# Retention's projections paced over the steps of the RWKV recurrence, and its states passed through DRAM

## The chip, the cores and the metric

One core of a Trainium2 chip runs one program. The metric is its device time in microseconds (us). PE, DVE, ACT, POOL and SP are the core's five instruction queues: TensorE (matmuls), VectorE, ScalarE, GpSimd and SyncE (which here only issues DMAs). Each queue runs its instructions in the order in which the program holds them, and an instruction that waits holds up everything behind it on its queue.

## The reference, cut to what matters

The whole computation is two transformer blocks. The change touches one layer of the second block, for 1024 latent rows and 256 context rows with 8 heads of 64. Two mixers start from the same normalised input `h`:

```python
u = h @ w_in                      # projections of every mixer, 1024 columns in
# retention, both directions: chunks of 128 rows, decay g per head
kv = einsum('bhnsd,bhnse->nbhde', kc * k_decay, vc)
s_next = g_chunk * s + kv_n       # state before each chunk: 64 x 64 per head
y = (q k^T * dmat) v + (q * q_decay) s_prev
# RWKV-7, both directions, row after row
s = s * w_t + (s @ -kk_t) (kk_t * a_t)^T + v_t k_t^T ;  y_t = s r_t
# combine: norm of each, times silu(u[gate columns]), then @ w_out
```

## The kernel before

All matrix products with weights are float32 work done as three matmuls on split operands (`mm3`, lines 217 to 219): `hi` and `lo` parts of the input, `hhi`/`hlo`, against those of the weights, `whi`/`wlo`. The input has three blocks of rows: blocks 0 and 1 hold 512 latent rows each, block 2 the 256 context rows. One projection of 8 depth slices is 24 matmuls: 256 columns wide in `proj_tm` (128 rows of input against 256 weight columns), 512 wide in `proj_fm` for blocks 0 and 1, 256 wide for block 2. Their PSUM tiles are called `pf` in this stage.

`mixers` runs the stage. `rwkv` is written first: the recurrence as 10 batches, each of two directions with two chunks of 64 rows, so 40 steps in all. For a batch `prep2` builds the operands (`wkr`, `wbk`, `wam`), `invert` inverts unit triangular matrices on DVE in 31 pairs of operations (`wtm`, lines 1670 and 1671) between two trips through DRAM (`wlt`, `wrd`), `merge` joins the halves (matmuls at lines 1694 and 1701), and `chain` makes the four steps. A step is five groups of 8 small matmuls (lines 1746, 1753, 1767, 1779, 1784), with ACT, DVE and POOL between them; its first is at line 1746, and its result leaves by `wyt` (line 1787). The operands of batch b+2 use the buffers of batch b, so the last part of `prep2` of b+2 waits for the end of the chain of b, and so in turn `invert`, `merge` and the chain of b+2.

Written behind it, and so of lower priority, is retention: `ret_proj` for block 0, 1 and 2 (60 projections for k, v and q, 24 for the gates `zt`), then `ret_state`: a table of decays (`rdm`), and for ten chunks the products k v for 8 heads (line 1370) and the two state recurrences on POOL (lines 1382, 1383), all kept in SBUF in one tile `rS`. A scheduler places the instructions of each queue by its own estimate of times and by priority, so the projections land between the steps of the recurrence wherever it believes PE to be free. Only one block of the input fits in SBUF here; the tiles of a new block are loaded from DRAM (line 1508) when the old one is done. After the recurrence `mix_tile` runs for ten tiles of 128 rows (loads of q, k, v at lines 1394 to 1398, transposes at line 1409).

Of the kernel before, what the change touches and what calls it, by code (L numbers as in the profile page):

```python
# [21 lines left out]
P = 128  # L22
# [17 lines left out]
class Ker:  # L40
# [1222 lines left out]

    def ret_proj(self, p, blocks):
# [55 lines left out]
    def ret_state(self, p, pl):  # L1320
# [3 lines left out]
        lg = p.tile([P, 16], F32, name="rlg")  # L1324
# [3 lines left out]
        tc_ = p.tile([P, 8], F32, name="rtc")  # L1328
        nc.sync.dma_start(tc_, a["c_rtc"])
        qdec = p.tile([P, 8, 2], F32, name="rqdec")  # L1330
        kdec = p.tile([P, 8, 2], F32, name="rkdec")
        gch = p.tile([P, 8], F32, name="rgch")
        for dd in range(2):
            l8 = lg[:, 8 * dd:8 * dd + 8]
            nc.vector.tensor_scalar(qdec[:, :, dd], l8, tc_[:, dd:dd + 1], None, op0=OP.mult)
            nc.vector.tensor_scalar(kdec[:, :, dd], l8, tc_[:, 2 + dd:3 + dd], None, op0=OP.mult)
            rows = slice(64 * dd, 64 * dd + 64)
            nc.scalar.activation(gch[rows], lg[rows, 8 * dd:8 * dd + 8], AF.Exp, scale=128.0)
# [3 lines left out]
        dm = p.tile([P, 8, P], F32, name="rdm")  # L1342
        rel = pl.tile([P, 4, P], F32, name="rrel", tag="rrel", bufs=1)
        nc.sync.dma_start(rel, a["c_rrel"])
        for h in range(8):
            e2 = pl.tile([P, 2, P], F32, name="re2", tag="re2", bufs=2)
# [3 lines left out]
            nc.gpsimd.tensor_add(dm[:, h], e2[:, 0], e2[:, 1])  # L1350

        S_ = p.tile([P, 10, 8, 64], F32, name="rS")
        nc.gpsimd.memset(S_[0:64, 8], 0.0)
        nc.gpsimd.memset(S_[64:128, 9], 0.0)

        nxt = [{8: 9, 9: 0}, {9: 8, 8: 7}]
        for t in range(7):
            nxt[0][t] = t + 1
            nxt[1][t + 1] = t
        for t in [8, 9] + list(range(8)):  # L1360
            k = pl.tile([P, 8, 64], F32, name="rkl", tag="rkl", bufs=2)
            nc.sync.dma_start(k, k_d[t].rearrange("p (h d) -> p h d", d=64))
            v = pl.tile([P, 512], F32, name="rvl", tag="rvl", bufs=2)
            nc.sync.dma_start(v, v_d[t])
            kd = pl.tile([P, 8, 2, 64], F32, name="rkd", tag="rkd", bufs=2)
            for dd in range(2):
                nc.gpsimd.tensor_mul(kd[:, :, dd], k, kdec[:, :, dd:dd + 1].to_broadcast([P, 8, 64]))
            ps = self.pf()
            for h in range(8):
                nc.tensor.matmul(ps[:, 64 * h:64 * h + 64], kd[:, h].rearrange("p a d -> p (a d)"),  # L1370
                                 v[:, 64 * h:64 * h + 64], start=True, stop=True)
            for dd in range(2):
                rows = slice(64 * dd, 64 * dd + 64)
                if t in nxt[dd]:
                    nc.scalar.copy(S_[rows, nxt[dd][t]].rearrange("p h d -> p (h d)"), ps[rows])
        for dd, t0 in ((0, 8), (1, 9)):
            rows = slice(64 * dd, 64 * dd + 64)
            t = t0
            while t in nxt[dd]:
                n = nxt[dd][t]  # L1380
                tm = pl.tile([P, 8, 64], F32, name="rtm", tag="rtm", bufs=2)
                nc.gpsimd.tensor_mul(tm[rows], S_[rows, t], gch[rows, :, None].to_broadcast([64, 8, 64]))
                nc.gpsimd.tensor_add(S_[rows, n], S_[rows, n], tm[rows])
                t = n
        self.rt = qdec, dm, S_

    def mix_tile(self, p, pe, t, cat, cv):
# [3 lines left out]
        qdec, dm, S_ = self.rt  # L1391
# [6 lines left out]
        nc.sync.dma_start(v, self.rv_d[t])  # L1398
        yield
# [28 lines left out]
        for h in range(8):  # L1428
            o = y[:, 64 * h:64 * h + 64]
            nc.tensor.matmul(o, sD[:, h % 2, h // 2], v[:, 64 * h:64 * h + 64], start=True, stop=False)  # L1430
            nc.tensor.matmul(o, qdT[:, h], S_[:, t, h], start=False, stop=True)
# [56 lines left out]
    def mixers(self):  # L1488
# [6 lines left out]
        with self.pool("rwm") as p, self.pool("rpb") as pb:  # L1495
# [4 lines left out]
            self.ret_tables(pb)  # L1500
            self.kept = {}
            for b in range(3):
                if b:
                    n = 512 if b < 2 else 256
                    hT = tuple(self.hA.tile([P, KD, 512], F32R, name="h" + x, tag=f"h{x}", bufs=1)[:, :, :n]
                               for x in ("hi", "lo"))
                    for t, src in zip(hT, self.nT_d[b]):
                        self.nc.sync.dma_start(t.bitcast(F32), src)
                    self.nT[b] = hT
                self.ret_proj(pb, [b])  # L1510

            self.close_all("wp", "hA")
            ers = ExitStack()
            rst = ers.enter_context(self.pool("rst", side=self.ms))
            with self.pool("rsl", side=self.ms) as pl:
                self.ret_state(rst, pl)
# [4 lines left out]
        with ers, self.pool("ret") as pr:  # L1521
# [3 lines left out]
            cat = [self.alloc_hT(b) for b in range(3)]  # L1525
            with self.pool("eop") as pe:
# [21 lines left out]
    def rwkv(self, p):  # L1548
        nc, a, dr = self.nc, self.a, self.dr
        d_ = self.rwd  # L1550
        ordt = [[8, 9] + list(range(8)), [9, 8] + list(range(7, -1, -1))]
# [166 lines left out]
        def chain(d, m, end):  # L1718
# [4 lines left out]
            for n, c in enumerate(cs):  # L1723
# [19 lines left out]
                for i in range(4):  # L1743
                    for e in range(2):
                        o = 512 * (1 - e) + 64 * i
                        nc.tensor.matmul(u[RW[e], o:o + 64], am[c][:, e, i, 0:64], xv[:, i, e],
                                         start=True, stop=True, tile_position=(0, 64 * e))
# [890 lines left out]
```

## Time and profile before

| | us |
|---|---|
| three timed runs | 4215.55, 4213.84, 4200.82 |
| their median | 4213.84 |
| the profiled execution | 4202.26 |
| its span | 4199.8 |

The profile is of one further execution. The span runs from its first to its last instruction, and the 2.5 us around it are start and end. The stage of the change lies from about 2099 us to 2934 us of the span: the recurrence's first step begins at 2248.4 us, its last result is stored at about 2928 us, and `mix_tile` follows. A time such as 2248.4 is always counted from the start of the span.

### The profile page before, as it was taken

The numbers are of one execution on the slowest core, as the hardware profiler recorded it, in microseconds if no ns is written. First come the engines' busy times: TensorE is split into PE (matmuls) and PEld (weight loads), VectorE is DVE, ScalarE is ACT, GpSimd is POOL, SyncE is SP. The second block draws the span as 40 slices with busy tenths as digits, with TensorE's granted clock in tenths as the row PEclk, the third lists the DMA queues.
The fourth block names the chain that finished last, engine by engine and source line by source line (L and its number), as shares of the span: only waits on it lengthen the run. The fifth ranks groups of instructions, "written<-read, shape, count | busy, mean of one in ns | idle before, by whom it ended". The sixth has DMA issues, their size and how long they took to land. (4 is left out here: it accounts for less than half of the span.)

```text
span 4199.8 us, 59342 instructions
## 1 busy us (share of the span) xinstructions
PE 3812.9 (91%) x23289; PEld 3077.8 (73%) x23289; DVE 2130.2 (51%) x3284; ACT 1320.4 (31%) x2641; POOL 1129.9 (27%) x1153
## 2 busy tenths in 40 slices
PE   7999989988999999789879899887889999998997
PEld 4788877776878788667767687776567877776775
DVE  4232434447343434644337686665556427653576
ACT  4333332215312121442233333332224224332211
POOL 1110202123101011202256343236431200003674
PEclk8999979998999999988989999876899999998998
DMA  5321227573141413333477655653754644324465
GB/s 201 123 100 67 98 84 264 189 263 118 50 148 63 147 50 129 126 125 122 138 229 221 187 161 173 206 157 99 234 188 142 225 134 125 102 70 152 165 203 193
DMA packets 453574, 627.03 MB, mean 149 GB/s; under 512 B 142577, under 2 KB 302499, under 8 KB 447152
## 3 DMA queue, kind: packets, MB, share of 16 engines
q1 hardware_dynamic: 402816, 421.50, 31.1%
q0 software_dynamic: 50480, 201.75, 14.5%
q8 instruction: 184, 3.01, 0.3%
q14 instruction: 94, 0.77, 0.1%
HBM read 427.27 MB, written 195.19 MB: 148 GB/s over the span
## 5 line engine op out<-in xcount | busy, mean ns | idle before, releaser
L217 PE MATMUL p<-hhi,whi 128*128 128x512 f32 x1056 | 415.8, 394 | 5.9 <-DVE hf L389 5.8
L218 PE MATMUL p<-hlo,whi 128*128 128x512 f32 x1056 | 414.3, 392 | 4.3 <-DVE hlo L391 4.3
L219 PE MATMUL p<-hhi,wlo 128*128 128x512 f32 x1056 | 413.8, 392 | 0.0
L217 PE MATMUL pf<-whi,hhi 128*128 128x512 f32 (+1 forms) x992 | 359.0, 362 | 29.4 <-ACT rqr L1279 9.4
L218 PE MATMUL pf<-wlo,hhi 128*128 128x512 f32 (+1 forms) x992 | 352.4, 356 | 3.7 <-DVE wlo L177 3.4
L177 DVE TENSOR_TENSOR wlo<-wraw,whi 128x2048 fp32r<-128x2048 f32 (+1 forms) x103 | 212.3, 2062 | 273.8 <-ACT whi L176 267.8
L219 PE MATMUL pf<-whi,hlo 128*128 128x512 f32 (+1 forms) x992 | 349.3, 353 | 0.0
L176 ACT CAST whi<-wraw 128x2048 fp32r<-128x2048 f32 (+1 forms) x123 | 193.2, 1575 | 459.6 <-PE pt L219 174.7
L217 PE MATMUL pf<-hhi,whi 128*128 128x512 f32 (+1 forms) x640 | 252.4, 394 | 6.0 <-DVE zt L1311 2.1
L218 PE MATMUL pf<-hlo,whi 128*128 128x512 f32 (+1 forms) x640 | 252.0, 394 | 0.0
L219 PE MATMUL pf<-hhi,wlo 128*128 128x512 f32 (+1 forms) x640 | 249.4, 390 | 0.0
L217 PEld LDWEIGHTS pf<-whi,hhi 128*128 128x128 f32 x992 | 198.7, 200 | 68.2 <-issue 14.1
L217 PE MATMUL pj<-whi,hhi 128*128 128x512 f32 (+1 forms) x560 | 216.5, 389 | 26.5 <-ACT whi L176 12.1
L217 PEld LDWEIGHTS p<-hhi,whi 128*128 128x128 f32 x1056 | 200.4, 190 | 54.1 <-DVE hf L389 6.2
L218 PEld LDWEIGHTS p<-hlo,whi 128*128 128x128 f32 x1056 | 200.2, 190 | 46.3 <-DVE hlo L391 5.3
L219 PEld LDWEIGHTS p<-hhi,wlo 128*128 128x128 f32 x1056 | 200.0, 189 | 42.6 <-issue 0.8
L218 PEld LDWEIGHTS pf<-wlo,hhi 128*128 128x128 f32 x992 | 198.9, 200 | 28.9 <-issue 4.1
L219 PE MATMUL pj<-whi,hlo 128*128 128x512 f32 (+1 forms) x560 | 214.1, 383 | 3.0 <-DVE hlo L381 3.0
L218 PE MATMUL pj<-wlo,hhi 128*128 128x512 f32 (+1 forms) x560 | 215.1, 384 | 0.2 <-DVE wlo L177 0.2
L219 PEld LDWEIGHTS pf<-whi,hlo 128*128 128x128 f32 x992 | 198.5, 200 | 22.1 <-issue 1.3
L1670 DVE TENSOR_TENSOR wtm<-wT,wL 128x2 f32<-128x2 f32 (+30 forms) x310 | 145.7, 470 | 37.5 <-POOL wL L1661 28.0
L217 PEld LDWEIGHTS pf<-hhi,whi 128*128 128x128 f32 x640 | 122.9, 192 | 37.9 <-issue 6.7
(750 smaller groups left out, 8544.6 us busy)
## 6 DMA issues: line engine op xcount, KB each, us to landing
wraw<-w_in POOLq DMA_DIRECT2D x25, 1024.0 KB, 6.0
wraw<-w_ada POOLq DMA_DIRECT2D x24, 1024.0 KB, 8.5
wraw<-w_up POOLq DMA_DIRECT2D x22, 1024.0 KB, 6.0
whi<-wkh POOLq DMA_DIRECT2D x40, 512.0 KB, 5.6
wlo<-wkl POOLq DMA_DIRECT2D x40, 512.0 KB, 5.2
wraw<-ada_w POOLq DMA_DIRECT2D x32, 512.0 KB, 4.5
ox<-x SPq DMA_DIRECT2D x48, 256.0 KB
xp<-xl SPq DMA_DIRECT2D x48, 256.0 KB
```

Of the source, the lines that this page charges most:

```text
L176: nc.scalar.copy(hi[:, :n], raw[:, :n])
L177: self.we.tensor_sub(lo[:, :n], raw[:, :n], hi[:, :n].bitcast(F32))
L217: mm(out, L[0], R[0], start=first, stop=False)
L218: mm(out, L[0], R[1], start=False, stop=False)
L219: mm(out, L[1], R[0], start=False, stop=last)
L1670: nc.vector.tensor_mul(tv, T[:, r0:, i:], L[:, i:i + 1, i:].to_broadcast([P, 16 - r0, n]))
```

## The change

- In `rwkv` the first matmul of each step is remembered in `self.marks` (40 of them).
- `paced` gives each projection of retention an edge on PE's queue: it may not stand before a given step's first matmul. The steps are dealt out by the sum of assumed durations (2.9 for a projection that is 256 wide, 5.45 for 512): the first 70 us of them are free, the rest is spread evenly over the 40 steps.
- The gates leave `ret_proj` and become `ret_gates`, which runs after k, v and q of all blocks, over blocks 2, 1, 0. Between gate projections `ret_state` advances by one round.
- `ret_state` handles four heads at a time: two passes of nine rounds. A round loads k and v of two chunks from DRAM (four DMAs), scales k on POOL, makes 8 pairs of head and direction as 64 x 64 matmuls, multiplies the state on POOL and adds on DVE; each state goes to DRAM by two DMAs. The table `rdm` goes through DRAM as well.
- `mix_tile` loads its chunk's state (256 KB), and the table once.
- `ctx_norm` stores block 0 of the input to DRAM too, since the gates need it again at the end: two more reloads.

```diff
@@ ctx_norm
-        for b in (1, 2):
+        for b in range(3):
@@ ret_proj and what was its end
+    def paced(self, us):
+        n = int((self.filled - self.lead) / self.pace)
+        self.filled += us
+        return self.tc.issue_after(self.marks[min(n, len(self.marks) - 1)]) if n >= 0 else nullcontext()
...
-                self.proj_tm(self.nT, W, 256, mk(dst, c0), tiles)
+                for t in tiles:
+                    with self.paced(2.9):
+                        self.proj_tm(self.nT, W, 256, mk(dst, c0), [t])
+
+    def ret_gates(self, p, blocks):
...
-                self.proj_fm(self.nT, W, c, ev_z((c0 + c) // P), blocks)
+                for b in blocks:
+                    with self.paced(5.45 if b < 2 else 2.9):
+                        self.proj_fm(self.nT, W, c, ev_z((c0 + c) // P), [b])
+                    yield
@@ ret_state
+        self.st_d = [self.dr.tile([P, 2, 256], F32, name=f"rst{t}") for t in range(10)]
+        for g in range(2):
+            S_ = pl.tile([P, 4, 64], F32, name="rS", tag="rS", bufs=2)
+            for n in range(10):
+                for dd in range(2):
+                    rows = slice(64 * dd, 64 * dd + 64)
+                    nc.sync.dma_start(self.st_d[order[dd][n]][rows, g], S_[rows].rearrange("p h d -> p (h d)"))
+                k = pl.tile([P, 2, 4, 64], F32, name="rkl", tag="rkl", bufs=1)
+                v = pl.tile([P, 2, 256], F32, name="rvl", tag="rvl", bufs=1)
+                for x, x_d in ((k.rearrange("p a h d -> p a (h d)"), k_d), (v, v_d)):
+                    for dd in range(2):
+                        nc.sync.dma_start(x[:, dd], x_d[order[dd][n]][:, 256 * g:256 * g + 256])
+                nc.gpsimd.tensor_mul(k, k, kdec[:, :, 4 * g:4 * g + 4, None].to_broadcast([P, 2, 4, 64]))
+                for h in range(4):
+                    for dd in range(2):
+                        nc.tensor.matmul(ps[64 * dd:64 * dd + 64, 64 * h:64 * h + 64], k[:, dd, h],
+                                         v[:, dd, 64 * h:64 * h + 64], start=True, stop=True, tile_position=(0, 64 * dd))
+                nc.gpsimd.tensor_mul(tm, S_, gch[:, 4 * g:4 * g + 4, None].to_broadcast([P, 4, 64]))
+                nc.vector.tensor_add(S_, tm, ps[:, :256].rearrange("p (h d) -> p h d", d=64))
+                yield
@@ mix_tile
+        S_ = p.tile([P, 8, 64], F32, name="rSl", tag="rSl", bufs=3)
+        nc.sync.dma_start(S_, self.st_d[t].rearrange("p g (h d) -> p (g h) d", d=64))
@@ mixers
+            self.filled, self.lead, self.pace = 0.0, 70.0, 215.0 / len(self.marks)
...
+            with self.pool("rzb") as pb, self.pool("rsl") as pl:
+                steps = self.ret_state(pl)
+                for b in (2, 1, 0):
+                    if b < 2:
+                        block(b)
+                    for _ in self.ret_gates(pb, [b]):
+                        next(steps, None)
+                self.run(steps)
@@ rwkv, chain
+                        if not i and not e:
+                            self.marks.append(mm.ins)
```

What this does to the order of instructions is shown at three places. The first is PE's queue in batch 0, from the first matmuls of its second step on (line 1746 before, 1774 in the changed kernel). Names without a number are tiles of the recurrence; `pf` are retention's projections. Before:

```order
L1746 MATMUL p_14598<-wxv,wam 64x64 x8
L217 MATMUL pf<-hhi,whi 128x512
L218 MATMUL pf<-hlo,whi 128x512
L217 MATMUL pf<-hhi,whi 128x512
L218 MATMUL pf<-hlo,whi 128x512
L219 MATMUL pf<-hhi,wlo 128x512
L217 MATMUL pf<-hhi,whi 128x512
```

and now:

```order
L1774 MATMUL p_14599<-wxv,wam 64x64 x8
L1774 MATMUL p_14659<-wxv,wam 64x64 x8
L1664 MATMUL pj<-ident,wbk 128x128 x4
L1670 MATMUL pj<-wkr,wbk 128x128 x4
L1783 MATMUL p_14599<-wrs,wX_0_13939 64x64 x8
L1783 MATMUL p_14659<-wrs,wX_0_13941 64x64 x8
L1797 MATMUL p_14599<-wxv,wbt 64x64 x8
L1797 MATMUL p_14659<-wxv,wbt 64x64 x8
```

Before, 19 projection matmuls stood between the first matmuls of two neighbouring steps; now the two steps stand next to each other and no projection is between them.

The second place is PE's queue at the end of the recurrence: its last two groups (lines 1779 and 1784 before, 1809 and 1814 now) and what follows. Before:

```order
L1753 MATMUL p_20019<-wrs,wX_1_13941 64x64 x8
L1779 MATMUL p_20019<-wS,wrr 64x64 x8
L1784 MATMUL p_20019<-wxv,wam 64x64 x8
L405 MATMUL pf<-ident,colr 128x8
L282 MATMUL pa<-wraw,cT_7260 32x512 x2
L1409 MATMUL pf<-ident,rql 128x128 x4
```

and now:

```order
L219 MATMUL pf<-hhi,wlo 128x512
L217 MATMUL pf<-hhi,whi 128x512
L1809 MATMUL p_20020<-wS,wrr 64x64 x8
L1814 MATMUL p_20020<-wxv,wam 64x64 x8
L218 MATMUL pf<-hlo,whi 128x512
L219 MATMUL pf<-hhi,wlo 128x512
L217 MATMUL pf<-hhi,whi 128x512
```

Before, the transposes of `mix_tile` (line 1409) followed the last step; now 98 projection matmuls, all 512 wide, stand between the last step and them.

The third place is POOL's queue where the rounds of `ret_state` begin (`rkl` and `rtm` are the round's, `wfc` and `wS` are what a step of the recurrence needs from POOL). Before, the rounds stood behind one another near the end:

```order
L1367 TENSOR_TENSOR rkd<-rkl,rkdec 128x8x64 x2
L1383 TENSOR_TENSOR rS<-rS,rtm 64x512
L1661 MEMSET wL 128x32
L1382 TENSOR_TENSOR rtm<-rS,rgch 64x512
L1367 TENSOR_TENSOR rkd<-rkl,rkdec 128x8x64 x2
L1383 TENSOR_TENSOR rS<-rS,rtm 64x512
```

and now:

```order
L1762 TENSOR_TENSOR wfc<-wfi 128x4
L1383 TENSOR_TENSOR rtm<-rS,rgch 128x256
L177 TENSOR_TENSOR wlo<-wraw,whi 128x1024
L1376 TENSOR_TENSOR rkl<-rkl,rkdec 128x512
L165 DMA wraw<-even_w_in 128x8x128
L1767 TENSOR_TENSOR wS<-wt_17687,wfc 128x256
L1767 TENSOR_TENSOR wS<-wt_17749,wfc 128x256
L1762 TENSOR_TENSOR wfc<-wfi 128x4 x2
```

The scaling of the loaded k (line 1376, which waits for its DMA) now stands ahead of operations that steps of the recurrence wait for (lines 1762 and 1767).

## Rows read from the trace of the kernel before

**Rows 1.** Busy time by stretch: batches 0 to 7, batch 8, batch 9, mix_tile.

```profile
core 0: us, PE busy (x) PEld busy (x) DVE busy (x) ACT busy (x) POOL busy (x), PEclk, DMA share, GB/s
2248.40:2842.90 594.50, 524.17 (x5929) 450.17 (x5928) 419.06 (x892) 221.63 (x571) 238.25 (x380) 0.90 0.61 182
2842.90:2907.00 64.10, 49.48 (x593) 45.70 (x592) 45.86 (x88) 16.95 (x38) 49.92 (x46) 0.54 0.26 67
2907.00:2928.00 21.00, 13.54 (x288) 11.76 (x288) 8.74 (x17) 6.63 (x18) 8.09 (x10) 0.86 0.22 61
2934.00:3100.00 166.00, 144.59 (x1111) 100.52 (x1111) 101.34 (x174) 47.97 (x90) 84.87 (x88) 0.86 0.72 226
```

**Rows 2.** The same, instructions that touch pf tiles alone: batches 0 to 7, batch 8.

```profile
2248.40:2842.90 594.50, 286.50 (x1567) 237.99 (x1566) 14.37 (x24) 29.68 (x68) 0.90 0.61 182
2842.90:2907.00 64.10, 25.54 (x113) 24.34 (x112) 0.00 (x0) 8.11 (x14) 0.54 0.26 67
```

**Rows 3.** Lines 1787, 1670, 1686, 1746, 1787: ns (min/median/max), first and last start.

```profile
L1787 ACT COPY wyt<-p x2: 360/364/367, 2450.9 to 2451.3; 64x256 f32<-64x256 f32 x2
...
L1670 DVE TENSOR_TENSOR wtm<-wT,wL x31: 160/292/730, 2471.6 to 2511.4; 128x2 f32<-128x2 f32 x1, 128x3 f32<-128x3 f32 x1, 128x8 f32<-128x8 f32 x1, 128x10 f32<-128x10 f32 x1
...
L1686 SPq DMA_DIRECT2D wV<-wrd x8: 303/448/1837, 2522.0 to 2529.4; - x8
...
L1746 PE MATMUL p<-wxv,wam x64: 222/222/347, 2536.6 to 2577.1; 128*64 128x64 f32 x64
...
L1787 ACT COPY wyt<-p x8: 348/366/367, 2549.3 to 2593.5; 64x256 f32<-64x256 f32 x8
```

**Rows 4.** Line 1746 in batches 0, 8 and 9, and line 1787 in batch 9.

```profile
L1746 PE MATMUL p<-wxv,wam x64: 222/222/369, 2248.4 to 2295.5; 128*64 128x64 f32 x64
...
L1746 PE MATMUL p<-wxv,wam x64: 314/314/369, 2842.9 to 2899.9; 128*64 128x64 f32 x64
...
L1746 PE MATMUL p<-wxv,wam x64: 222/222/369, 2907.0 to 2922.3; 128*64 128x64 f32 x64
...
L1787 ACT COPY wyt<-p x8: 365/366/367, 2914.2 to 2927.7; 64x256 f32<-64x256 f32 x8
```

**Rows 5.** Chain of waits by line, as a share of 2250:2770 and of 2840:2928.

```profile
by line: DVE wtm L1670 9.0%; DVE wT L1671 6.4%; DMA wV<-wrd 6.1%; DMA wlt<-wam 5.8%; PE pf L217 5.8%; PE pf L218 5.2%; PE pf L219 5.1%; issue 4.4%; PE pj L1642 3.7%; DMA wrd<-wT 3.5%; DVE wam L1644 3.3%; DVE wxv L1738 2.6%; DMA hhi<-nTd2h 2
...
by line: DVE wtm L1670 26.1%; DVE wT L1671 12.4%; PE p L1779 7.0%; PE p L1784 7.0%; DMA wrd<-wT 4.9%; DVE wt L1772 4.9%; issue 4.2%; PE pf L1370 4.1%; SPq L1686 4.0%; PE p L1753 3.4%; PE p L1767 3.2%; DMA rvl<-rv 3.0%; ACT wyt L1787 2.5%; D
```

**Rows 6.** Timeline of PE: neighbouring projection matmuls, 512 and 256 wide (start, us).

```profile
2629.10 0.40 PE L218 MATMUL pf<-hlo,whi 128*128 128x512 f32 x1
2629.34 0.39 PE L219 MATMUL pf<-hhi,wlo 128*128 128x512 f32 x1
...
2362.68 0.28 PE L218 MATMUL pf<-wlo,hhi 128*128 128x256 f32 x1
2362.79 0.28 PE L217 MATMUL pf<-whi,hhi 128*128 128x256 f32 x1
```

**Rows 7.** Operations of ret_state by line; then one step group on the timeline.

```profile
L1370 PE MATMUL pf<-rvl,rkd x160: 421/421/476, 2824.6 to 2892.9; 128*128 128x64 f32 x160
...
L1367 POOL TENSOR_TENSOR rkd<-rkl,rkdec x20: 1040/1048/1375, 2818.4 to 2881.8; 128x512 f32<-128x512 f32 x20
...
L1383 POOL TENSOR_TENSOR rS<-rS,rtm x18: 1254/1262/1521, 2837.9 to 2911.6; 64x512 f32<-64x512 f32 x18
...
2633.26 0.64 PE L1746 MATMUL p<-wxv,wam 128*64 128x64 f32 x16
```

**Rows 8.** PE waiting for a reloaded block (timeline); a load in the chain of waits.

```profile
2644.91 0.55 PE L217 MATMUL pf<-whi,hhi 128*128 128x256 f32 x1 [5.80 <-DMA hhi<-nTd2h]
...
2886.86 2.64 DMA rvl<-rv
```

**Rows 9.** The loads and first transposes of mix_tile.

```profile
L1394 SPq DMA_DIRECT2D rql<-rq x10: 320/354/613, 2929.3 to 3042.2; - x10
...
L1409 PE MATMUL pf<-ident,rql x40: 272/273/476, 2933.1 to 3061.5; 128*128 128x128 f32 x40
```

More of the change, by code (lines that the diff above doesn't have):

```diff
@@ L1 @@
 import math
-from contextlib import ExitStack
+from contextlib import ExitStack, nullcontext
 import numpy as np
@@ L1349, in ret_state @@
             nc.gpsimd.tensor_mul(e2, e2, rel[:, 2:4])
[L1350 to L1385, printed above, removed]
+            dm = pl.tile([P, P], F32, name="rdm", tag="rtm", bufs=1)
+            nc.gpsimd.tensor_add(dm, e2[:, 0], e2[:, 1])
+            nc.sync.dma_start(self.dm_d[:, h], dm)
+        self.qdec = qdec
     def mix_tile(self, p, pe, t, cat, cv):
         nc = self.nc
-        qdec, dm, S_ = self.rt
+        qdec, dm = self.qdec, self.dm
         py = lambda: self.ps.tile([P, 512], F32, name="py", tag="py", bufs=2)
@@ L1430, in mix_tile @@
             nc.tensor.matmul(o, sD[:, h % 2, h // 2], v[:, 64 * h:64 * h + 64], start=True, stop=False)
-            nc.tensor.matmul(o, qdT[:, h], S_[:, t, h], start=False, stop=True)
+            nc.tensor.matmul(o, qdT[:, h], S_[:, h], start=False, stop=True)
         cols = slice(t * P, t * P + P)
@@ L1494, in mixers @@
         self.open_ps(2)
-        with self.pool("rwm") as p, self.pool("rpb") as pb:
+        with self.pool("rwm") as p:
             self.rwkv(p)
@@ L1499, in mixers, with block @@
             self.we = self.nc.gpsimd
-            self.ret_tables(pb)
             self.kept = {}
[L1502 to L1510, printed above, removed]
+            self.filled, self.lead, self.pace = 0.0, 70.0, 215.0 / len(self.marks)
+            def block(b):
+                n = 512 if b < 2 else 256
+                hT = tuple(self.hA.tile([P, KD, 512], F32R, name="h" + x, tag=f"h{x}", bufs=1)[:, :, :n]
+                           for x in ("hi", "lo"))
+                for t, src in zip(hT, self.nT_d[b]):
+                    self.nc.sync.dma_start(t.bitcast(F32), src)
+                self.nT[b] = hT
+            with self.pool("rpb") as pb:
+                self.ret_tables(pb)
+                for b in range(3):
+                    if b:
+                        block(b)
+                    self.ret_proj(pb, [b])
+            with self.pool("rzb") as pb, self.pool("rsl") as pl:
+                steps = self.ret_state(pl)
+                for b in (2, 1, 0):
+                    if b < 2:
+                        block(b)
+                    for _ in self.ret_gates(pb, [b]):
+                        next(steps, None)
+                self.run(steps)
             self.close_all("wp", "hA")
[L1513 to L1516, printed above, removed]
         self.ms, self.ss = "left", "right"
@@ L1520, in mixers @@
         self.open_ps(2, 1)
-        with ers, self.pool("ret") as pr:
+        with self.pool("ret") as pr:
             self.open_hA()
@@ L1525, in mixers @@
             cat = [self.alloc_hT(b) for b in range(3)]
+            self.dm = pr.tile([P, 8, P], F32, name="rdml")
+            self.nc.sync.dma_start(self.dm, self.dm_d)
             with self.pool("eop") as pe:
@@ L1550, in rwkv @@
         d_ = self.rwd
+        self.marks = []
         ordt = [[8, 9] + list(range(8)), [9, 8] + list(range(7, -1, -1))]
@@ L1745, in chain @@
                         o = 512 * (1 - e) + 64 * i
-                        nc.tensor.matmul(u[RW[e], o:o + 64], am[c][:, e, i, 0:64], xv[:, i, e],
-                                         start=True, stop=True, tile_position=(0, 64 * e))
+                        mm = nc.tensor.matmul(u[RW[e], o:o + 64], am[c][:, e, i, 0:64], xv[:, i, e],
+                                              start=True, stop=True, tile_position=(0, 64 * e))
+                        if not i and not e:
+                            self.marks.append(mm.ins)
                 rs = p.tile([P, 256], F32, name="wrs", tag=f"wrs{d}", bufs=1)
```

28 lines of the change are left out of this document (18 added, 10 removed).

## The prediction

> **What bounds the kernel now.** I read the busy time by stretch first, then the order of instructions, then single lines of the recurrence. In batches 0 to 7 PE is busy for 524 of 594.5 us at a granted clock of 0.90, so nearly always; tiles `pf`, retention's, take 286 us of it [rows 1, 2]. DVE is busy for 419. In batch 8 the projections are over: the clock is 0.54 (PE runs mostly at 1.2 GHz), and the state work of retention takes 25.5 of PE's 49.5 us, while POOL is busy for 50 of 64 [rows 1, 2]. Batch 9 takes 21 us with nothing beside it.
>
> The recurrence itself is a loop over two batches, since the operands of batch b+2 wait for the end of the chain of b. One pass of it: the chain of batch 2 ends at 2451.3 + 0.4 = 2451.7; the inversion for batch 4 starts at 2471.6 and its last product at 2511.4; its result is back in SBUF after loads issued until 2529.4; the first step begins at 2536.6 and the last result leaves at 2593.5 + 0.4 = 2593.9 [rows 3]. That is 142 us for two batches: 20 for the rest of the preparation and its trip through DRAM, 40 of inversion, 25 of trips and joining, 57 for the chain. The chain alone needs no more than 2928 - 2907 = 21 us, as batch 9 shows [rows 4]; in batch 4 it takes 57, because projections and other batches' work stand between its instructions. The chain of waits agrees: in 2250:2770 the three lines of projections have 5.8 + 5.2 + 5.1 = 16% of 520 us, 84 us or some 12 us of each of the 7.2 batches, and the inversion's two lines another 15% [rows 5]. So fill on PE costs the recurrence time, but not as much as it lasts (286 / 8 = 36 us a batch).
>
> **Part by part.** All sums start from the profiled execution, 4202.3 us.
>
> Prices first. At the full clock a 512-wide projection matmul follows the last after 0.23 us, a 256-wide one after 0.11 [rows 6]; with 24 of them a projection takes 5.5 or 2.75 us. A state matmul of the new form (64 x 64) has the shape of a step's: 8 in 0.64 us, so 0.08 each, where the old form with 128 weight columns costs 2 x 0.23 at the low clock (16 profiled rows or 8 matmuls in 3.7 us) [rows 7].
>
> *Batches 0 to 7.* I counted in the listings what stands on PE between the first matmul of a batch's chain and its last. Before: 342 matmuls 512 wide and 859 256 wide, 342 x 0.23 + 859 x 0.115 = 177 us. Now: 59 and 855, and 71 state matmuls, 13.6 + 98.3 + 5.7 = 118 us. The difference is 60 us. What stands between two chains hardly changes (42 and 275 before, 37 and 279 now). Each chain lies in one of two interleaved loops, the even batches' and the odd ones', so a microsecond taken out of a chain moves the end by about half a microsecond. I take **-30**. If the fill is not on the path at all it is 0; if PE's time alone counted it would be -60.
>
> *Batch 8.* The old state work goes: 25.5 us of PE at the low clock, and on POOL most of 20 x 1.05 + 18 x 1.26 = 44 us for `rkd` and `rS` alone, spread from 2818 to 2912 [rows 7]. In comes fill: 96 x 0.23 + 40 x 0.08 = 25 us. The rest of PE's work, 24 us at 0.54, shrinks to some 13 with the clock held up. PE then has 38 instead of 49.5 us of work: **-10**, bounds -20 (POOL was the brake) and +15 (fill goes on top as it does on an idle path).
>
> *Batch 9.* It had no fill; now 94 projection matmuls (94 x 0.23 = 21.6 us) and 16 state matmuls (1.3 us) stand among its steps. PE was idle for 21 - 13.5 = 7.5 us [rows 1], which hides some: **+17**, bounds +14 and +24.
>
> *After the last step.* 98 matmuls follow, 98 x 0.23 = **+22**. Nothing covers them: the loads and transposes of `mix_tile` stand behind them (before, the first load was issued at 2929.3, the first transpose ran at 2933.1 [rows 9]), and its tiles lie where weights and input of the projections lay. Their evacuation and store add the same few microseconds that the recurrence's last store had, so I count no more.
>
> *Reloads.* Four blocks are loaded instead of two. One reload before held PE for 5.80 us [rows 8], and PE's order puts the recurrence behind it. Two more: **+6**, bounds 0 and 12. The extra store of block 0 falls in a stretch where nothing is bound by DMA; I count 0, and at most 4 MB at the 226 GB/s of [rows 1], 18 us, if the next weights queue behind it.
>
> *State rounds.* 18 rounds, each 6 DMAs on SP, 1.05 us on POOL for k [rows 7] and about half that for the state, one addition on DVE. POOL's scaling waits for a load and stands ahead of `wfc` and `wS`, for which the next step's DVE and PE work waits. A load of this kind that was waited for took 2.64 us [rows 8]. If all 18 waits fell on the path: 18 x 2.64 = 48; if all rounds lie in gaps: 0. Loads are issued well ahead in most rounds, so I stay near the low end: **+5**.
>
> *mix_tile.* Ten more loads of 256 KB and a table of 512 KB: 3.1 MB, at 226 GB/s 14 us of DMA. DMA is at 0.72 there and PE busy for 145 of 166 us [rows 1], so most is covered, except at the start, when everything is loaded at once: **+4**, bounds 0 and 14.
>
> Sum: -30 - 10 + 17 + 22 + 6 + 5 + 4 = **+14 us**. The profiled execution, 4202.3, lies near the low end of what was timed; the mean of it and the three runs is 4208.1. With +14 that is **4222 us**, 0.2% above the median of 4213.8. A difference of 0.5% (21 us) is about what a measurement of this kernel can tell from no change, so I forecast none that is clear.
>
> **The rivals.**
>
> *A, faster: PE's own time is the bound.* PE busy for 88% of batches 0 to 7 [rows 1] speaks for it: then each microsecond of fill that leaves a batch shortens the batch by as much, the total of fill is unchanged, and the stage gains the idle and half-clock time of its tail. Batches 0 to 7 give -60 instead of -30 and batch 8 -15: 4222 - 35 = 4187 us. Against it: batch 8, with less PE work than any before it, still took 64 us. Chance 0.22. [...]
>
> *B, slower: latency is the bound, not fill.* If the loop of inversion, trips and DVE queue sets the pace (the inversion alone is 40 of the 71 us that a batch has in the pass of [rows 3], and batch 8, free of projections, still took 64), then the first term is 0 and the fill at the end is paid in full: 4222 + 30 = 4252 us. It decides, with a clear loss, once the first term is smaller than 17 of its 30 us. Against it: 16% of the chain of waits is fill [rows 5]. Chance 0.23.
>
> *C, slower: the rounds of retention hold POOL and SP.* Every round's wait on the path, +48 instead of +5: 4265 us. For it: in-order queues, and one buffer each for k and v. Against it: they are loaded while PE works on other things. Chance 0.10.
>
> That the change does nothing is excluded: the listings show the projections moved.
>
> **How the numbers follow.** My forecast has 0.40, A 0.22, B 0.23, C 0.10, and 0.05 is for what I have not seen. Around the forecast the terms' bounds leave about 4200 to 4244. The range that leaves out 2 in 10 goes from a little below A to B and most of C: 4182 to 4262. Faster by over 0.5% (below 4193) are most of A and little else: 0.22. Slower by over 0.5% (above 4235) are most of B, nearly all of C and an eighth or more of the forecast's own: 0.37. Between them 0.41.
>
> **What the changed kernel's profile would show.** Batches 0 to 7 tell most: 594.5 / 8 = 74.3 us each before; right at about 70.5, A at 67 or less, B at 74. Batch 8 at a clock above 0.85 and below 64 us; batch 9 at some 38 us; then 22 us of projections with PE busy throughout, and the first transpose some 5 us behind. Waits of POOL's line 1376 for `rkl` that add up to over 20 us would speak for C. I am wrong if a batch stays at 74 us, or falls below 66.

## The result and the profile after

The changed kernel takes **4266.69 us** (median of 4 runs, 4263.14 to 4267.92) beside 4210.68 for the kernel before: ratio **1.0137, 95% interval 1.0121 to 1.0153**, slower by 1.4%. The forecast was 4222, its range 4182 to 4262.

Busy time by stretch in the changed kernel, as in [rows 1]: batches 0 to 7, batch 8, batch 9, from the last result to `mix_tile`'s first load, and 166 us of `mix_tile`.

```profile
core 0: us, PE busy (x) PEld busy (x) DVE busy (x) ACT busy (x) POOL busy (x), PEclk, DMA share, GB/s
2255.10:2852.40 597.30, 500.48 (x5771) 434.32 (x5770) 418.55 (x886) 206.47 (x538) 223.07 (x355) 0.81 0.59 173
2852.40:2907.40 55.00, 47.91 (x622) 38.71 (x624) 40.64 (x101) 11.95 (x30) 15.14 (x23) 0.84 0.66 205
2907.40:2957.50 50.10, 43.76 (x465) 34.71 (x462) 10.54 (x22) 12.16 (x33) 14.16 (x22) 0.87 0.57 194
2957.50:2985.80 28.30, 22.26 (x89) 16.73 (x88) 3.51 (x6) 4.37 (x9) 7.93 (x15) 0.96 0.63 209
2985.80:3151.80 166.00, 145.69 (x1014) 102.77 (x1015) 90.85 (x150) 44.09 (x83) 77.17 (x84) 0.81 0.76 238
```

The same for tiles `pf` alone in batches 0 to 7 and in batch 9, as in [rows 2].

```profile
2255.10:2852.40 597.30, 226.46 (x1407) 195.48 (x1406) 10.56 (x23) 20.33 (x52) 0.81 0.59 173
2907.40:2957.50 50.10, 29.81 (x145) 21.69 (x142) 3.15 (x6) 1.77 (x3) 0.87 0.57 194
```

Batches 0 to 7 hold 60 us less of `pf` work (226 against 286) and last as long as before. The clock fell with that work, from 0.90 to 0.81, and PE's other work there grew from 524 - 286 = 238 to 500 - 226 = 274 us: 36 of the 60 us came back at once.

Batch 8 came out as forecast (55 us against 64 before). In batch 9 whole projections stand between the groups of a step. PE's timeline there:

```profile
2937.02 0.64 PE L1774 MATMUL p<-wxv,wam 128*64 128x64 f32 x16
2937.59 0.50 PE L217 MATMUL pf<-hhi,whi 128*128 128x512 f32 x1
...
2942.71 0.39 PE L218 MATMUL pf<-hlo,whi 128*128 128x512 f32 x1
2943.03 0.68 PE L1783 MATMUL p<-wrs,wX 64*64 64x64 f32 x16
```

Behind the last projection PE waits for `mix_tile`'s first load (timeline of PE; line 1423 is the transpose of [rows 9]):

```profile
2981.63 0.39 PE L219 MATMUL pf<-hhi,wlo 128*128 128x512 f32 x1
2981.95 0.22 PE L405 MATMUL pf<-ident,colr 8*128 8x8 f32 x1
2989.68 1.12 PE L1423 MATMUL pf<-ident,rql 128*128 128x128 f32 x4 [7.52 <-DMA rql<-rq]
```

POOL's scaling of k (line 1376) in 2607:2960, first its duration, then its waits:

```profile
L1376 POOL TENSOR_TENSOR rkl<-rkl,rkdec x18: 1036/1045/1583, 2644.4 to 2932.3; 128x512 f32<-128x512 f32 x18
its engine sat idle before it (us, times) until:
  DMA rkl<-rk: 32.4, 8
```

The spans differ by 4265.0 - 4199.8 = 65.2 us: first step later by 6.7, batches 0 to 7 +2.8, batch 8 -9.1, batch 9 +29.1, from the last result to `mix_tile`'s first load +27.0, from there to the end +8.7.

### The profile page after: what moved, and what is told of

Its sections match the earlier page's. It is cut to its first block, busy times and chain, and to the rows that moved or that the text cites. A ratio compares the mean times of both kernels' runs of the same rounds, so it can differ in the third digit from the quotient of the medians.

```text
span 4265.0 us, 59783 instructions
## 1 busy us (share of the span) xinstructions
PE 3857.0 (90%) x23417; PEld 3111.9 (73%) x23417; DVE 2134.2 (50%) x3302; ACT 1309.8 (31%) x2623; POOL 1090.5 (26%) x1133
## 3 DMA queue, kind: packets, MB, share of 16 engines
q1 hardware_dynamic: 417104, 444.58, 32.1%
## 5 line engine op out<-in xcount | busy, mean ns | idle before, releaser
L217 PEld LDWEIGHTS p<-hhi,whi 128*128 128x128 f32 x1056 | 200.5, 190 | 54.6 <-DVE hf L389 6.8
L218 PEld LDWEIGHTS p<-hlo,whi 128*128 128x128 f32 x1056 | 200.2, 190 | 46.2 <-DVE hlo L391 5.3
L218 PEld LDWEIGHTS pf<-wlo,hhi 128*128 128x128 f32 x992 | 202.4, 204 | 32.1 <-issue 4.8
```

Of the source, the lines that this page charges most:

```text
L217: mm(out, L[0], R[0], start=first, stop=False)
L218: mm(out, L[0], R[1], start=False, stop=False)
```

## The experiments

The label of a run stands for the edit that is shown with its expectation below. The stretches are read from the first starts of the chain's and `rql`'s lines and the end of the last `wyt` in each run's trace. "to mix" is from the last result to `mix_tile`'s first load (negative: the load came first), "rest" from there to the end. Stretches are of one execution each; where the code is the same, batches 0 to 7 still vary by some 10 us (two executions of the changed program: 597 and 592), and "rest" by 16 (e14 and e16 are one program: 1276 and 1292), so a difference of a few us there means nothing. The traces of e15 and e16 are of their shortest and longest execution (4161.1 and 4223.0 us).

| run | time, us | ratio (95%) | batches 0-7 | 8 | 9 | to mix | rest |
|---|---|---|---|---|---|---|---|
| before | 4210.7 | | 594.5 | 64.1 | 21.0 | 1.3 | 1270.5 |
| changed | 4266.7 | 1.0137 (1.0121-1.0153) | 597.3 | 55.0 | 50.1 | 28.3 | 1279.2 |
| e1 | 4256.7 | 1.0119 (1.0094-1.0145) | 591.9 | 54.6 | 46.2 | 26.9 | 1283.4 |
| e2 | 4268.3 | 1.0133 (1.0099-1.0167) | 598.4 | 54.1 | 50.2 | 26.5 | 1289.5 |
| e3 | 4326.9 | 1.0284 (1.0240-1.0327) | 584.6 | 54.0 | 39.9 | 140.4 | 1259.4 |
| e4 | 4272.3 | one run | 535.0 | 50.7 | 42.5 | 120.0 | 1293.9 |
| e5 | 4225.3 | 1.0041 (1.0025-1.0056) | 631.7 | 58.2 | 22.0 | 1.3 | 1271.5 |
| e6 | 4643.1 | one run | 539.2 | 53.1 | 25.8 | 514.3 | 1283.5 |
| e7 | 4255.2 | 1.0106 (1.0072-1.0140) | 592.7 | 56.6 | 47.1 | 19.7 | 1272.9 |
| e8 | 4582.0 | one run | 507.3 | 43.0 | 25.9 | 510.2 | 1280.3 |
| e10 | 4228.0 | 1.0040 (1.0021-1.0059) | 594.2 | 48.7 | 38.6 | -7.2 | 1300.3 |
| e11 | 4616.7 | one run | 531.2 | 48.3 | 26.2 | 503.1 | 1282.3 |
| e12 | 4644.8 | one run | 540.1 | 51.3 | 26.1 | 511.6 | 1282.8 |
| e13 | 4242.6 | 1.0083 (1.0066-1.0099) | 600.0 | 70.5 | 37.5 | -7.5 | 1284.4 |
| e14 | 4192.5 | 0.9979 (0.9964-0.9993) | 591.2 | 47.7 | 38.4 | -16.6 | 1276.3 |
| e15 | 4171.7 | 0.9928 (0.9913-0.9942) | 576.3 | 49.3 | 21.7 | 1.3 | 1260.3 |
| e16 | 4190.2 | 0.9977 (0.9959-0.9994) | 598.4 | 50.8 | 37.0 | -15.1 | 1292.0 |
| e0 | 4213.6 | 1.0013 (0.9998-1.0028) | 583.4 | 80.1 | 27.4 | 1.5 | 1271.7 |
| c1 | 4260.8 | 1.0125 (1.0091-1.0158) | 587.9 | 52.9 | 38.8 | 84.8 | 1244.7 |
| c2 | 4243.5 | 1.0083 (1.0067-1.0098) | 595.6 | 69.2 | 34.8 | 28.3 | 1268.4 |

**Do the queue edges do anything?** The first run spreads the projections over 30 steps, the second drops the edges.

```diff
-            self.filled, self.lead, self.pace = 0.0, 70.0, 215.0 / len(self.marks)
+            self.filled, self.lead, self.pace = 0.0, 70.0, 215.0 / 30
```

> The changed kernel with the projections spread over the first 30 of the 40 steps instead of all 40. Theory 1 (the loop of inversion, trips and waits of DVE sets the batch period in batches 0 to 7; fill on PE costs little there, but in full where it stands after the last step and in batch 9): batches 0 to 7 stay near 597 us, batch 9 falls from 50 to about 21 to 25, the stretch after the last result from 28 to about 5; total near 4215 us, ratio to before 1.000 to 1.003. Theory 2 (fill costs the batches about half of what it lasts, and spreading did gain, but the state rounds, the reloads and the lower clock gave it back): the 48 us of fill that move into batches 0 to 7 cost some 25 to 30 there; total near 4240, ratio 1.006 to 1.009.

```diff
-        return self.tc.issue_after(...) if n >= 0 else nullcontext()
+        return nullcontext()
```

> The changed kernel without the queue edges that pace the projections; everything else of the change stays (states beside the gates, through DRAM, gates of block 0 last). Theory 1: like the run with 30 steps, total 4205 to 4220. Theory 2: batches 0 to 4 go back from 352 to about 361 us and batches 5 to 7 keep their 245; batch 9 and the tail fall as in the other run; total 4220 to 4235.

Neither theory's numbers held. With 30 steps the scheduler's order is the changed kernel's on every engine, instruction for instruction: these edges bound nothing, and the run is one more timing of the same program (10 us below the first, which is what chance can do between two such medians). Without edges the trace shows the same order too, by line and tile name, on every engine, and the time does not move. So the spread comes from the projections' order (gates last, k, v and q one after the other), not from the edges.

**What do rounds last, and less fill on PE, do?**

```diff
                     for _ in self.ret_gates(pb, [b]):
-                        next(steps, None)
+                        pass
                 self.run(steps)
```

> The changed kernel with all 18 state rounds and the decay table issued after the last gate projection instead of one round beside each. Theory 1: the rounds cost the batches nothing, so batches 5 to 7 stay near 245 us, and 18 rounds in a row at 3 us or more come on top at the end: total 4310 to 4330. Theory 2: batches 5 to 7 fall from 245 to about 234 and batch 8 by a few us, with the same 55 or more at the end: total 4295 to 4315.

POOL's scaling of k in 2800:3100 of this run:

```profile
L1376 POOL TENSOR_TENSOR rkl<-rkl,rkdec x17: 1042/1042/1045, 2928.0 to 3036.7; 128x512 f32<-128x512 f32 x17
its engine sat idle before it (us, times) until:
  DMA rkl<-rk: 32.1, 17
```

Batches 5 to 7 fell from 245 to 237, near theory 2's 234, but the total, 4326.9, is in theory 1's range; the 13 us in batches 0 to 7 are little more than two executions differ by. Batch 9 fell by 10. What neither theory had: with nearly nothing beside them 17 rounds take (3036.7 - 2928.0) / 16 = 6.8 us each, not 3. A round waits for its loads (32.1 us in all here), and its loads for the round before, whose buffers they use.

```diff
@@ kernel before: proj_tm, proj_fm, while retention's projections run
-            for k in range(KD):
+            kk = 2 if self.cut else KD
+            for k in range(kk):
```

> The kernel before with only a quarter of the matmuls of each of retention's projections (2 of 8 slices of the contraction); weights, evacuations, rotation and stores stay, so retention's values are not the reference's. Theory 1: batches 0 to 7 fall by less than 40 us, to 555 or more. Theory 2 and my forecast's step (fill among a chain's instructions costs half of what it lasts): three quarters of the 177 us of fill inside the chains, halved, are 66 us, so about 528. If PE's own time counted, about 200 us less, near 400.

Batch 0 of the kernel before, then batch 0 and batches 1 to 7 of this run:

```profile
2248.40:2317.60 69.20, 65.86 (x727) 54.13 (x726) 48.13 (x87) 28.21 (x63) 39.74 (x47) 0.99 0.73 220
2239.40:2342.10 102.70, 70.39 (x634) 54.01 (x633) 70.81 (x125) 35.91 (x80) 49.98 (x66) 0.63 0.79 257
2342.10:2871.10 529.00, 400.32 (x4246) 335.09 (x4245) 367.03 (x781) 189.26 (x495) 234.87 (x353) 0.66 0.55 157
```

No theory had this: with a quarter of the matmuls the batches got *longer*, 631.7 us, at a clock of 0.66. Of the 37 us 33 are in batch 0 (102.7 us against 69.2 before), where DMA moves 257 GB/s against 220; that the weights and evacuations of the shorter projections, which come in faster bursts there, are the reason is argued, not shown. Batches 1 to 7 last as long as before (529 against 525) with most of the fill gone.

**What does fill cost the recurrence?** e6 puts all projections behind the last step; e11 and e12 add the loop below, matmuls that nothing reads, N = 8 or 24 behind each of the first 32 steps.

```diff
-            self.filled, self.lead, self.pace = 0.0, 70.0, 215.0 / len(self.marks)
+            self.filled, self.lead, self.pace = 0.0, -1e6, 215.0 / len(self.marks)
+            for mk in self.marks[:32]:
+                with self.tc.issue_after(mk):
+                    ps = self.pf()
+                    for i in range(N):
+                        self.nc.tensor.matmul(ps, hi[:, i % KD, 0:P], hi[:, i % KD, :], ...)
```

> The changed kernel with every projection queued behind the last step (282 us of them), so that the recurrence runs alone. Theory 1: the recurrence alone is nearly as slow as with fill, batches 0 to 7 at 520 us or more. Theory 2: a chain takes 21 us as batch 9 of the kernel before does, the loop of two batches 20 + 40 + 25 + 21 = 106 us, batches 0 to 7 about 425. Behind it some 290 us of projections in both.

> The recurrence alone (all projections behind the last step), with 8 matmuls 512 wide that nothing reads queued behind each of the first 32 steps: 256 x 0.23 = 59 us of PE at full clock, no DMA, no evacuation. Alone, batches 0 to 7 took 539 us with the recurrence's own matmuls at 397 us of PE and the clock at 0.59. If the clock is what fill pays with (own matmuls get shorter as it rises): own matmuls fall to 300 to 350, batches 0 to 7 at 515 to 545. If load on PE only costs (half of what it lasts): 539 + 30 to 60 = 570 to 600.

> The same with 24 matmuls behind each of the 32 steps: 768 x 0.23 = 177 us of PE, about what the changed kernel's projections put into batches 0 to 7. If the clock pays for it: own matmuls fall from 397 to 240 to 280 us, batches 0 to 7 at 540 to 565. If load on PE costs half of what it lasts: 539 + 88 = 627. What the changed kernel has above this run (597) is then weights, evacuations, reloads and rounds.

Busy time in batches 0 to 7 of e6, e11 and e12 (a fence each), with the `pf` tiles' part under it for the last two:

```profile
2225.50:2764.70 539.20, 396.98 (x4362) 327.30 (x4362) 379.80 (x865) 182.01 (x472) 82.62 (x155) 0.59 0.26 61
```

```profile
2223.80:2755.00 531.20, 414.87 (x4620) 332.79 (x4620) 382.41 (x865) 181.33 (x475) 90.75 (x155) 0.72 0.26 63
2223.80:2755.00 531.20, 88.84 (x256) 57.10 (x256) 0.00 (x0) 0.00 (x0) 0.72 0.26 63
```

```profile
2231.10:2771.20 540.10, 496.77 (x5130) 394.87 (x5130) 385.08 (x867) 180.13 (x473) 93.06 (x155) 0.85 0.26 61
2231.10:2771.20 540.10, 207.82 (x768) 148.40 (x768) 0.00 (x0) 0.00 (x0) 0.85 0.26 61
```

The spans of all three came out as theory 1 and the clock had it (e12's own matmuls stayed above the 240 to 280 us expected). Alone, the recurrence needs 539 us; with 208 us of extra PE work 540. PE's other work falls from 397 to 497 - 208 = 289 us as the clock rises from 0.59 to 0.85, and the rest fits into idle time. So matmuls of fill, together with the clock that comes with them, cost next to nothing (-8 us for 89 us of them, +1 for 208). Whether they would cost something at a fixed clock, which the faster clock gives back, no run separates. What the real fill costs, 55 to 58 us, about the same in both kernels, lies by elimination in what comes with its matmuls: weights, evacuations, rotation on POOL, reloads and stores (DMA 0.6 instead of 0.26, POOL 223 to 238 us instead of 83); these I did not separate.

**Is it the inversion?** Every other pair of the 31 is left out, in the changed kernel and in e6.

```diff
-            for i in range(30, -1, -1):
+            for i in range(30, -1, -2):
```

> The changed kernel with every other pair of DVE instructions of the inversion left out (16 of 31 columns done), so that the recurrence's numbers are not the reference's. Theory 1 (the loop of inversion, trips and chain sets the period): an inversion falls from 46 to about 24 us, the loop over two batches from 143 to some 121, batches 0 to 7 from 597 to 500 to 530. Theory 2 (PE's fill sets it): 580 or more. The projections then come later against the steps, so more of them stands behind the last step (76 instead of 22 us); only batches 0 to 7 are compared.

> The recurrence alone (all projections behind the last step) with every other pair of the inversion's DVE instructions left out, so that its numbers are not the reference's. Alone it took 335 us for batches 0 to 4 and 204 for 5 to 7, with DVE busy for 70 in 100 and the granted clock at 0.60. If DVE's queue sets the pace (each inversion of 38 us falls to 21 or less, of which DVE is busy 22 less): batches 0 to 7 fall from 539 by 80 to 130, to 410 to 460. If PE at half clock sets it: 500 or more.

In e4 batches 0 to 7 fall by 62 us, to just above the range expected, with 40 us less fill among them. Alone it is 32 us, where 80 to 130 were expected: at 507 us e8 lies where the expectation had PE at half clock set the pace. Against that speaks e12, where the clock rose to 0.85 and the time stayed; but e12 has 208 us of fill on PE besides, so the clock is not excluded. An inversion takes 21 us in e8, from its first product to its last, and its result is back some 13 us before the chain ahead ends (in batches 2 to 8, but for batch 5), yet a chain lasts 58 to 59 us in e6 and 59 to 62 in e8 (means over batches 2 to 4 and 5 to 7), with no fill at all, against 21 in batch 9 [rows 4]. The inversion is a part; what else holds a chain is seen in e6's timeline:

```profile
2498.37 0.16 DVE L1698 TENSOR_TENSOR wtm<-wT,wL 128x2 f32<-128x2 f32 x1 [2.62 <-POOL wL L1689]
2498.52 2.41 POOL L1650 TENSOR_TENSOR wbk<-wlkd,wem 64x512 f32<-64x512 f32 x2
2498.56 0.15 DVE L1699 TENSOR_REDUCE wT<-wtm 128x1 f32<-128x2 f32 x1
2498.75 0.95 DVE L1698 TENSOR_TENSOR wtm<-wT,wL 128x3 f32<-128x3 f32 x1
2498.83 0.38 ACT L1789 ACTIVATE wxv<-p 64x256 f32<-64x256 f32 x1 [0.40 <-PE p L1783]
2499.74 0.16 DVE L1699 TENSOR_REDUCE wT<-wtm 128x1 f32<-128x3 f32 x1
2499.93 1.02 DVE L1698 TENSOR_TENSOR wtm<-wT,wL 128x8 f32<-128x8 f32 x1
...
2502.32 0.68 DVE L1639 TENSOR_TENSOR wkr<-wlkap,wep 128x512 f32<-128x512 f32 x1
2502.92 0.69 DVE L1640 TENSOR_TENSOR wkr<-wlr,wep 128x512 f32<-128x512 f32 x1
...
2503.62 1.38 DVE L1648 SCALAR_TENSOR_TENSOR wbk<-wlba,wem 64x512 f32<-64x512 f32 x2
2504.92 0.42 DVE L1791 TENSOR_SCALAR wxv<-p 64x256 f32<-64x256 f32 x1
...
2505.15 1.09 PE L1664 MATMUL pj<-ident,wbk 128*128 128x128 f32 x4 [6.36 <-DVE wbk L1648]
...
2508.17 1.12 PE L1797 MATMUL p<-wxv,wbt 128*64 128x64 f32 x16
```

The two halves of `wxv` wait for the same group of matmuls. ACT's (line 1789) runs at 2498.83; DVE's (line 1791) at 2504.92, six us later, behind pairs of the inversion and operands of the batch after next. The chain's next group (line 1797) needs both halves, and on PE's queue it stands behind transposes (line 1664) that waited for DVE as well. So DVE, which runs its queue in order and is busy for 380 of 539 us, holds the chain here. It is no single case: over 2300:2750 PE waited 29 us for line 1791.

```profile
L1797 PE MATMUL p<-wxv,wbt 128*64 128x64 f32 x432 | 28.1, 303 | 29.2 <-DVE wxv L1791 29.2
```

This is read from the trace; no run moved those operations.

**What do the states cost, what the loads?** In this order: no work in the rounds; k and v loaded once for each group of heads; no state loads in `mix_tile`; the first and the third together.

```diff
@@ e10, e14: ret_state
                 if n == 9:
                     break
+                yield
+                continue
@@ e13: ret_state
+                if not n:
                     k = pl.tile([P, 2, 4, 64], F32, name="rkl", tag="rkl", bufs=1)
...
@@ e7, e14: mix_tile
-        S_ = p.tile([P, 8, 64], F32, name="rSl", tag="rSl", bufs=3)
-        nc.sync.dma_start(S_, self.st_d[t].rearrange(...))
+        S_ = self.dm[:, :, 0:64]
```

> The changed kernel without the loads, scaling, matmuls and additions of the 18 state rounds (the states stay zero, their stores remain), so retention's part of the output is not the reference's. By the run with the rounds last, batches 5 to 7 fall by about 10 us to 235 and batch 9 by about 10 more than its projections; no projection stands behind the last step in this order (in the changed kernel 22 us of them), so total near 4266 - 10 - 10 - 25 = 4221. If the rounds cost nothing (my forecast's low end, +5 in all): batches 5 to 7 at 245, total 4240.

> The changed kernel with k and v of the state rounds loaded once for each group of heads instead of in each round, everything else of the rounds in place (the same k and v again and again, so the states are not the reference's). If the rounds cost through the waits for their loads (POOL waited 32 us for k between 2607 and 2957): near the run without rounds, 4225 to 4238. If through their operations and places in the queues: 4250 to 4265.

> The changed kernel without mix_tile's ten loads of the states (it takes a part of the decay table in their place, so the output is not the reference's). If these loads cost the 9 us that the time from mix_tile's first load to the end grew by, that part falls from 1279 to about 1270; if the late weights of the ada projections (first load at 2972 instead of 2922, behind the projections) cost it, it stays at 1279 to 1285.

> The changed kernel without the work of the state rounds and without mix_tile's loads of the states (a part of the decay table in their place, so retention's part of the output is not the reference's): what is left is the spread of the projections with its reloads, and the store of block 0. If the prices add up and the spread is worth nothing: 4228 - 11 = 4217, between 4211 and 4222, ratio 1.001 to 1.003. If the spread costs of its own (reloads, late weights): above 4225. If it gains as forecast (30 us in batches 0 to 7 and 10 in batch 8, less 17 in batch 9): below 4205.

The rounds cost 1.0137 - 1.0040, 41 us of 4208, near the first expectation's 45, but not where it put them: batches 0 to 7 did not shorten (594.2), and the gain lies in batches 8 and 9 and behind, where without rounds no projection is left over. Their loads are 1.0137 - 1.0083, 23 us of the 41: e13 lies between its two expectations, so both causes hold. Without the state loads e7 is 13 us shorter, on the side of the first of its two expectations, but its interval reaches 1.0140 and so takes in the changed kernel; clear of both intervals is e10 against e14, 1.0040 - 0.9979 or 26 us, where the rounds are empty. Without rounds' work and state loads, e14 came out in the branch "gains as forecast"; but it also lacks the state work that the kernel before does, which that expectation forgot. Hence e15, the kernel before without that work, and e14 once more on the same chip:

```diff
@@ e15: ret_state of the kernel before
-        for t in [8, 9] + list(range(8)):
+        for t in []:
...
-            while t in nxt[dd]:
+            while False:
```

> The kernel before without the loads, scaling, matmuls and recursion of its states (they stay zero), so retention's part of the output is not the reference's. Batch 8 falls from 64 to 45 to 53 us, nothing else moves: total 4208 - 11 to - 19, 4189 to 4197, the same as the run with the spread alone (4192.5) within 6 us, if the spread is worth nothing. If the spread gains 15 us or more, this run is at 4205 or above.

> The run with the spread alone once more, on the same chip as the kernel before without states: 4188 to 4198. The difference of the two is the worth of the spread with its reloads and the store of block 0.

e16 took 4190.2 (ratio 0.9977, 0.9959 to 0.9994). Busy time in batches 0 to 7, 8 and 9, first e14, then e15:

```profile
2253.40:2844.60 591.20, 504.99 (x5713) 435.24 (x5712) 411.31 (x881) 213.19 (x559) 217.38 (x357) 0.84 0.62 185
2844.60:2892.30 47.70, 43.35 (x546) 34.71 (x546) 36.78 (x97) 11.24 (x28) 7.45 (x15) 0.90 0.55 166
2892.30:2930.70 38.40, 31.20 (x393) 25.08 (x392) 9.49 (x21) 9.17 (x23) 7.66 (x10) 0.90 0.41 128
```

```profile
2250.50:2826.80 576.30, 508.04 (x5881) 435.10 (x5880) 412.01 (x885) 217.80 (x565) 229.07 (x366) 0.92 0.61 182
2826.80:2876.10 49.30, 24.91 (x448) 21.51 (x448) 36.11 (x94) 8.84 (x24) 3.73 (x7) 0.57 0.19 44
2876.10:2897.80 21.70, 15.45 (x320) 13.47 (x320) 7.40 (x16) 7.33 (x20) 2.72 (x4) 0.74 0.14 44
```

e15 fell below its expectation: the old state work is worth 33 us (4204.9 against 4171.7 on that chip), in its trace 11 us in batch 7 (63.6 against 74.9), where that work begins, 15 in batch 8 and 10 in the rest. The spread, with its reloads and the store, therefore costs 4190.2 - 4171.7 = 18 us; by the traces, with the scatter said above, batches 0 to 7 gain nothing, batch 8 lasts about the same with 18 us more PE work, and batch 9 pays 17 for its three projections. The new state work costs 1.0137 - 0.9977, some 67 us, against those 33.

**The store of block 0, and two other mixtures.**

```diff
@@ e0: kernel before, ctx_norm
-        for b in (1, 2):
+        for b in range(3):
@@ c1, c2: mixers, without edges (c1 as shown; c2 with b < 1, then gates of blocks 2 and 1, one round each)
+                        self.ret_proj(pb, [b])
+                        if b < 2:
+                            for _ in self.ret_gates(pz, [b]):
+                                pass
...
+                    for _ in self.ret_gates(pz, [2]):
+                        next(steps, None)
+                        next(steps, None)
```

> The kernel before with the one extra store of block 0 of the normalised input (4 MB of the change's additions) and nothing else. The first step began 4 to 7 us later in the changed kernel and its variants (2252 to 2255 against 2248). If the store is the reason (its traffic delays what is queued behind it): slower by 4 to 8 us, ratio 1.001 to 1.002, with the first step at 2252 to 2255. If it is hidden, as my forecast had it: ratio 0.999 to 1.001 and the first step at 2248.

> The states part of the change alone: no queue edges, each block's gate projections right behind its other projections as in the kernel before (no third and fourth reload), the 18 state rounds two at a time beside the gates of block 2, through DRAM. 10 us of projections stand behind the last step. If the loss of the change is fill moved to batch 9 and behind it (theory 1): batches 0 to 7 at 595 to 605, batch 8 about 50, batch 9 25 to 30, then 12; total near 4215, ratio 1.000 to 1.004. If rounds on POOL and SP are the loss: batch 8 and 9 stay at 64 and 40 or more; ratio 1.008 or more.

> A version put together from what the runs showed: no queue edges, the gates of block 0 right behind its other projections (one reload less), the state rounds beside the gates of blocks 2 and 1; all projections then stand ahead of step 38, none in batch 9's second half or behind it. By the prices measured so far: first step at 2252, batches 0 to 4 as in the kernel before (361), batches 5 to 7 as in the changed kernel (245), batch 8 about 60 with 33 us of projections, batch 9 about 28, then 5, and from mix_tile's first load to the end 1280: span 4231, ratio 1.006. If the projections behind the last step were the main loss and all else is free, it would be 4195 to 4205 and faster than both.

The store is worth 5 us (interval -1 to +12, so not clear of nothing), and the first step came at 2253.2, as the first expectation said; but e1, e2 and the changed kernel, which have one order, begin it at 2252.6, 2252.0 and 2255.1, so one such time tells little. c1 and c2 have 10 and 0 us of projections behind the last step and are slower than before all the same: the rounds then trail (85 and 28 us to `mix_tile`). c2 beats the changed kernel by 0.5% and misses its sum by some 10 us (ratio 1.0083 where 1.006 was expected). No run with the states' work done points to a version faster than the kernel before.

## Why the prediction was wrong

- **Batches 0 to 7, -30: the step that failed first.** That "a microsecond taken out of a chain moves the end by about half a microsecond" is wrong for matmuls. e12 adds 208 us of them for 1 us, and in the change 60 us less of them left 597.3 us where there were 594.5. The clock, which I had left as it was, moves with such work; besides, a chain waits on DVE and on DMA. How much each of the two gives is open. That a chain takes 57 us "because projections and other batches' work stand between its instructions" is half wrong: with no projection at all it takes 58 (e6). The chain of waits' 16% of fill [rows 5] named the last to release PE, not what would be saved. Rival B's first term, 0, is what was measured, and its sign too: 597.3 / 8 = 74.7 us a batch. Its cause was half right: DVE's queue, the inversion only in part. A, which had -60 there, is excluded. The Trainium skill ("Perfetto Trace Analysis", Identifying the Most-Contended Engine) says that the busy share of matmuls is not a good measure of how close TensorE is to its roofline, and names the busy share of weight loads as one that is to be used instead. That share was 450 / 594.5 = 76% in batches 0 to 7 [rows 1], and e12 agrees that PE had time to spare.
- **State rounds +5, mix_tile +4: mis-sized.** Rounds 41, state loads 13 to 26, together 67 against the 33 of the old state work, of which I had credited only batch 8's part. The 41 hold what stands behind the last step, which the forecast had as a term of its own (+22): no projection stands there when the rounds come last (e3), are empty (e10) or load only once for each group of heads (e13). I priced a round by waits in gaps; alone it lasts 6.8 us, and with one dealt out beside each gate projection seven of the eighteen fall into batches 8 and 9. That their length is what holds the projections back is argued from these orders. Rival C's sign came too: POOL waited 32 us for `rkl`, over the 20 named, and C's 4265 is near the result, reached by another sum.
- **Batch 8, -10:** right in size, clock 0.84. **Batch 9, +17:** 29; without rounds it is 17 (38.4 - 21.7). **After the last step, +22:** 27, with 7.5 us to the first transpose instead of 5.
- **Store of block 0, 0:** about 5, inside my bound. **Reloads, +6:** not separated.

Against the forecast's +14 the profiled execution has +65. By stretch the miss of 51 is 22 in batches 0 to 7 (with rounds and reloads), 12 in batch 9, 5 behind it, 5 in the rest, 7 before the first step and 1 in batch 8.

## What to carry to other kernels

Before work is moved off an engine's path, load that engine with work that nothing reads: if the time stays, moving that work gains nothing by itself. For TensorE such a test gives the net price, since the granted clock moves with the load. What the work costs then lies in what comes with it, transfers and evacuations above all (here by elimination). A serial chain of small rounds through DRAM is not priced by waits or busy time alone: look at how long a round lasts by itself (6.8 us here), and at what the rounds push behind the end. A planner's edge that bounds nothing leaves the order as it was, so compare the orders before crediting it.

## What the runs showed of the hardware

Extra PE work sped the recurrence's own matmuls up: 397 us of them at a granted clock of 0.59 (e6) became 289 at 0.85 (e12, PE's busy time less that of `pf`).

A DVE operation with two inputs in SBUF took 0.95 and 1.02 us, where its neighbours of the same kind took 0.16, while POOL's line 1650 ran (two operations); the second ended with it (2499.93 + 1.02 = 2500.95 against 2498.52 + 2.41 = 2500.93, e6's timeline above). The Trainium skill ("SBUF — State Buffer", Who interferes with whom) says that such a DVE operation and a GpSimd operation that reads SBUF exclude each other; these rows agree. A reduction with one input (line 1699, at 2498.56) took 0.15 us in the same time. What this costs over a batch was not measured.
